# Stick-breaking heads: the weight product as two fp32r products instead of one in fp32

## The chip, the cores and the metric

The kernel runs on one core of one Trainium2 chip. The metric is the device time of one execution in microseconds (us), as the median of several runs. The names of the engines below: PE is TensorE (matmuls), DVE is VectorE, ACT is ScalarE, POOL is GpSimd, SP is SyncE. PE writes its products into PSUM, eight banks of 512 fp32 columns for each of the 128 partitions; DVE and ACT read and write PSUM and SBUF.

## The reference, cut to what matters

Two transformer blocks run one after the other over 512 tokens of width 1024. The second has a mixer of three kinds of heads; the change is in its six stick-breaking heads of width 64:

```
z = einsum('bqhd,bkhd->bhqk', q_blk, k) * scale
log_beta = log_sigmoid(z)
log_stay = where(before, log_sigmoid(-z), 0.0)
tail = cumsum(log_stay, axis=3, reverse=True) - log_stay
weight = where(before, exp(log_beta + tail), 0.0)
out = einsum('bhqk,bkhd->bqhd', weight, v)
...
y = concatenate([y_a, y_b, y_c], axis=-1) @ w_out
x = x + (1.0 + gate1) * y
```

Here `before` keeps the keys that lie ahead of the query. `y_b` are these six heads (384 columns); `y_a` comes from a gating branch, `y_c` from dilated-window heads. A feed-forward layer follows.

## The kernel before

Activations lie transposed in SBUF, channels on partitions and the 512 tokens along the free dimension. A product of near-fp32 accuracy is made of fp32r products (fp32r is the one-pass format of PE): each operand is split into a high part (rounded to fp32r, a CAST) and a low part (the rest, a subtract), and `mm3` (lines 163 to 166) adds three products, high by high, low by high and high by low. `split_to` (lines 119 to 133) makes the two parts: the high part on ACT (line 126) or on DVE (line 124), the low part on DVE (line 131). Weights come from HBM on SP's queue in `slab` and are split there (`whi` on ACT, line 154, `wlo` on DVE, line 156).

The heads come in three pairs. `stick` (from line 1009) does one head. Keys lie on partitions in four blocks j of 128, and only queries at or behind the block are computed, so the blocks have 512, 384, 256 and 128 columns. They lie in three PSUM tiles `z` (t = 0: 512 columns; t = 1: 384; t = 2: 256 + 128). For each tile, from t = 2 to t = 0:

- PE makes z (two fp32r products for each block, line 1026, and a mask, line 1028).
- ACT makes softplus in three steps (Abs, line 1031; Exp and Ln through `act`, line 231), DVE finishes it (line 1034) and splits it (`sph`, `spl`, lines 124 and 131).
- DVE adds up what lies in later blocks (lines 1040 and 1043), ACT and DVE split it (`lah`, `lal`).
- PE subtracts the running sums from z (products with `negtri` and `negone`, line 1054).
- ACT takes Exp into an fp32 tile `w`, and PE multiplies it with the values, in fp32, into a bank `o` that both heads of the pair share (line 1060). The stationary operand is a window of 128 columns with one head's 64 value columns and 64 zeros, so that each head adds to its own 64 partitions.

After a pair, `split_to` turns `o` into two fp32r parts for the output product. The values tile `vn` is made by `values` (lines 822 to 828) from the bank of a token-wise product; it also holds the values of one dilated group.

Between the heads stand "fills": the output product of `y_a` and `y_c` (`w_out_ac`, eight blocks of 15 fp32r matmuls with 512 columns, `mm3` lines 164 to 166) and the splitting of two slabs of the next layer's weights. `FILL` says behind which head each fill stands in the program. The order on each engine isn't the program's: a scheduler sets it when the kernel is built, by its own estimate of times, by the tiles' buffers and by program order; on the chip each engine then runs its list in that order and waits by semaphores. The PSUM pool of this phase has one bank `ps`, six `z` and one `o`. `last_phase` (from line 1180) then adds the product of `y_b` with `w_out_b`: first three blocks of 512 columns, each with its three k steps in a row, then `gemm_last` in halves of 256 columns.

Of the kernel before, what the change touches and what calls it, by code (L numbers as in the profile page):

```python
# [22 lines left out]
T = 512  # L23
# [24 lines left out]
class Builder:  # L48
# [773 lines left out]
    def values(self, ps, npair, pool, tag):  # L822
# [4 lines left out]
        self.nc.scalar.copy(v[:, :, 0::2, :], ps[:, :npair * P].rearrange("p (r s c) -> p r s c", s=2, c=64))  # L827
        return t

    def by_rest(self, parts):  # L830

        cols = []
        for i, ps in enumerate(parts):
            t = self.t("sq", 2, self.tmp)
            (self.nc.vector.tensor_copy if i else self.nc.scalar.copy)(
                t.rearrange("p (c m) -> p c m", c=4), ps.rearrange("p (m c) -> p c m", c=4))
            cols.append(t)
        for c in range(4):
            ps = self.ps() if c % 2 == 0 else ps
            half = ps[:, 256 * (c % 2):256 * (c % 2) + 256]  # L840
            for i, t in enumerate(cols):
                self.nc.tensor.transpose(half[:, i * P:i * P + P], t[:, c * P:c * P + P], self.ident)
            yield half
# [74 lines left out]
    def dilated_values(self, vn, vp, y_pool):  # L918
        nc = self.nc
# [50 lines left out]
        for g in (1, 2, 0):  # L970
            out = self.ps() if g == 2 else self.ps("st", 1)
            banks = [[(b, b) for b in range(4)]] if g else [[(0, 0), (1, 0), (1, 1)], [(2, 1), (2, 2), (3, 2), (3, 3)]]
            for h in range(2):
                p, f = probs[2 * g + h], lse[g][:, 4 * h:4 * h + 4]
                if g:
                    v = p.rearrange("p (b c) -> p b c", b=4)
                    tt(v, v, f.unsqueeze(2).to_broadcast([P, 4, P]), ALU.mult)
                else:
                    o = 0
                    for b in range(4):  # L980
                        n = 128 if b == 0 else 256
                        nc.vector.tensor_scalar(p[:, o:o + n], p[:, o:o + n], f[:, b:b + 1], None, ALU.mult)
                        o += n
            o = 0
            for bank in banks:
                n = len(bank) * P
                pts = []
                for h in range(2):
                    ps = self.ps("sc", 3)
                    for i in range(len(bank)):  # L990
                        nc.tensor.transpose(ps[:, i * P:(i + 1) * P], probs[2 * g + h][:, o + i * P:o + i * P + P],
                                            self.ident)
                    pt = self.t("sq" if h else "rb", 2, self.tmp)
                    (nc.vector.tensor_copy if h else nc.scalar.copy)(pt[:, :n], ps[:, :n])
                    for i, (b, j) in enumerate(bank):
                        pts.append((b, j, h, pt[:, i * P:(i + 1) * P]))
                o += n
                for b in sorted({b for b, _ in bank}):
                    mine = [x for x in pts if x[0] == b]
                    for i, (_, j, h, pt) in enumerate(mine):  # L1000
                        v = self.window(vp[j], g - 1, h) if g else self.window(vn[j], 3, h)
                        nc.tensor.matmul(out[:, b * P:(b + 1) * P], v, pt, start=i == 0, stop=i == len(mine) - 1)
            if g:
                ys[g] = self.split(out.rearrange("p (c m) -> p c m", c=4), y_pool, "y", view=perm)
            else:
                ys[g] = self.split(out, y_pool, "y")
        return ys

    def stick(self, qh, ql, k, v, pair, h, out):


        nc = self.nc
        where = {0: (0, 0), 1: (1, 0), 2: (2, 0), 3: (2, 256)}
        sp = [None] * 3

        later = [None] * 4
        for t in (2, 1, 0):
# [44 lines left out]

    def part(self, n, tag, whole, rest, name, dt=F32R):

        return self.ph.tile([P, n], dt, tag=f"{tag}{n}", name=name, bufs=whole if n == T else rest)

    def mixer(self, stat):

# [5 lines left out]
        with ExitStack() as ctx:  # L1074
# [4 lines left out]
            with stat as cx:  # L1079
# [38 lines left out]
                kt_pool = self.pool("kt", 3, ctx, side="right")  # L1118
                self.ph = ph
                with cr:  # L1120
                    qk = self.dilated_qk(self.dilated_in(xs, 1), cos, sin, 1)
                    for g, after in ((1, 2), (2, 0), (0, None)):
                        mine, start = qk, self.tc.tile_snap_priority()
                        if after is not None:
                            parts = self.dilated_in(xs, after)
                        else:
                            vn = [self.values(ps, 4, vn_pool, "vn") for ps in
                                  self.gemm_tok(self.dr["w_vn"], xs, T, 2, lambda t, b: t[:, b * P:(b + 1) * P])]
                        with self.before(start):
                            self.dilated_scores(g, *mine)  # L1130
                        if after is not None:
                            qk = self.dilated_qk(parts, cos, sin, after)
                bqk = []
                for pr in range(3):
                    q, k = self.pair(self.dr["w_bqk"], pr, xs)
# [11 lines left out]
            with ExitStack() as ce:  # L1147
                self.psum = self.pool("psum_e", 6, ce, space=PSUM)
                self.ph = self.pool("ph_c2", 1, ce)
                self.bufs = {"ps": 1}  # L1150
                add = self.add_gated(16)
                ready = []

# [6 lines left out]
                        self.gemm(self.dr["w_out_ac"], y_a + y_c, add, (abs(i),), m=2 * abs(i), tag="z" if i < 0 else "ps")  # L1160

                for pr in range(3):
                    out = self.ps("o", 1)
                    for h in range(2):
                        self.stick(*bqk[pr][h], vn, pr, h, out)
                        for i in FILL[2 * pr + h]:
                            fill(i)
                    if pr < 2:
# [5 lines left out]
                    self.split_to(out, *y_b[-1])  # L1174
                for i in FILL[6]:
                    fill(i)
        self.bufs = {}
# [2 lines left out]
    def last_phase(self, y_b, wq, held, first, wf0, ctx):  # L1180

        with ctx:
# [9 lines left out]
            for m, k, pool in ((0, 3, ()), (3, 3, ()), (6, 2, (wq, D))):  # L1192
# [183 lines left out]
```

## Time and profile before

| | us |
|---|---|
| median of 3 runs | 1729.18 |
| lowest and highest run | 1727.09, 1729.4 |
| the profiled execution, whole | 1730.88 |
| its span in the trace | 1729.1 |
| PE busy | 1708.1 (99%) |
| DVE busy | 1123.8 (65%) |
| ACT busy | 709.3 (41%) |
| POOL busy | 54.0 (3%) |

The rows below come from this one execution; it lies 1.7 us above the median. Times in them are microseconds from the span's start. A row of the timeline tells when an instruction began and how long it lasted; the next on the same engine may begin before that end, since engines are pipelined, so what an instruction costs in a dense row is the distance of two starts. The heads' phase lies from 1268.5 to 1333.3 us.

### The profile page before, as it was taken

The numbers are of one execution on the slowest core, as the hardware profiler recorded it, in microseconds if no ns is written. First come the engines' busy times: TensorE is split into PE (matmuls) and PEld (weight loads), VectorE is DVE, ScalarE is ACT, GpSimd is POOL, SyncE is SP. The second block draws the span as 40 slices with busy tenths as digits, with TensorE's granted clock in tenths as the row PEclk, the third lists the DMA queues.
The fourth block names the chain that finished last, engine by engine and source line by source line (L and its number), as shares of the span: only waits on it lengthen the run. The fifth ranks groups of instructions, "written<-read, shape, count | busy, mean of one in ns | idle before, by whom it ended". The sixth has DMA issues, their size and how long they took to land.

```text
span 1729.1 us, 20582 instructions
## 1 busy us (share of the span) xinstructions
PE 1708.1 (99%) x8175; PEld 1426.2 (82%) x8175; DVE 1123.8 (65%) x1756; ACT 709.3 (41%) x1078; POOL 54.0 (3%) x97
## 2 busy tenths in 40 slices
PE   9999999999999999999999999999999999999998
PEld 7888887888888788887888888987788988888887
DVE  5655699537756478879963775676577766536644
ACT  4323334314434355543431443543466444314432
POOL 0000000000000110000000000012100000000000
PEclk9999999999999999999999999999999999999999
DMA  6222464222222232236423222414323022222221
GB/s 233 98 97 98 143 237 172 88 103 98 90 101 102 74 98 74 92 112 246 178 100 107 98 90 99 149 53 130 102 63 107 28 75 97 100 107 98 90 101 66
DMA packets 39472, 189.99 MB, mean 110 GB/s; under 512 B 5584, under 2 KB 6608, under 8 KB 27216
## 3 DMA queue, kind: packets, MB, share of 16 engines
q1 hardware_dynamic: 36000, 180.94, 29.9%
q0 software_dynamic: 2656, 6.30, 1.5%
q8 instruction: 64, 1.05, 0.2%
q10 hardware_dynamic: 720, 1.44, 0.2%
q14 instruction: 32, 0.26, 0.0%
HBM read 180.27 MB, written 2.10 MB: 105 GB/s over the span
## 4 chain that ended last, share of the span: by engine, by line
PE 88%; DVE 6%; DMA 3%; issue 1%; ACT 1%; DVEq 0%; POOLq 0%; POOL 0%; SPq 0%; ACTq 0%
PE ps L164 27%; PE ps L165 27%; PE ps L166 26%; DMA ada<-w_ada 2%; DVE ada L483 2%; DVE wlo L156 1%; DVE cv L283 1%; PE pt L164 1%; PE pt L165 1%; PE o L1060 1%; PE pt L166 1%; PE sc L674 1%; PE z L1054 1%; PE sc L907 0%; PE z L1026 0%
## 5 line engine op out<-in xcount | busy, mean ns | idle before, releaser
L165 PE MATMUL ps<-xsh,wlo 128*128 128x512 f32 (+1 forms) x1416 | 546.0, 387 | 1.7 <-DVE wlo L156 1.4
L166 PE MATMUL ps<-xsl,whi 128*128 128x512 f32 (+1 forms) x1416 | 542.6, 385 | 0.0
L164 PE MATMUL ps<-xsh,whi 128*128 128x512 f32 (+1 forms) x1416 | 540.9, 387 | 0.8 <-ACT xsh L128 0.6
L154 ACT CAST whi<-raw 128x1024 fp32r<-128x1024 f32 (+6 forms) x281 | 296.5, 1060 | 466.6 <-PE ps L166 390.1
L156 DVE TENSOR_TENSOR wlo<-raw,whi 128x1024 fp32r<-128x1024 f32 (+4 forms) x282 | 346.8, 1233 | 91.9 <-ACT whi L154 90.6
L165 PEld LDWEIGHTS ps<-xsh,wlo 128*128 128x128 f32 x1416 | 267.3, 189 | 58.0 <-DVE wlo L156 5.0
L164 PEld LDWEIGHTS ps<-xsh,whi 128*128 128x128 f32 x1416 | 267.2, 189 | 55.6 <-ACT xsh L128 1.4
L166 PEld LDWEIGHTS ps<-xsl,whi 128*128 128x128 f32 x1416 | 265.8, 188 | 52.5
L165 PE MATMUL ps<-hidh,wlo 128*128 128x512 f32 (+1 forms) x658 | 241.4, 367 | 0.0
L164 PE MATMUL ps<-hidh,whi 128*128 128x512 f32 (+1 forms) x658 | 241.3, 368 | 0.0
L166 PE MATMUL ps<-hidl,whi 128*128 128x512 f32 (+1 forms) x658 | 241.3, 367 | 0.0
L283 DVE SCALAR_TENSOR_TENSOR cv<-e,par,cv 128x511 f32<-128x511 f32 x192 | 142.0, 746 | 2.2 <-ACT cv L279 0.4
L164 PEld LDWEIGHTS ps<-hidh,whi 128*128 128x128 f32 x658 | 123.9, 188 | 20.6
L165 PEld LDWEIGHTS ps<-hidh,wlo 128*128 128x128 f32 x658 | 123.6, 188 | 20.7 <-DVE wlo L156 0.2
L166 PEld LDWEIGHTS ps<-hidl,whi 128*128 128x128 f32 x658 | 123.7, 188 | 20.4
L288 DVE TENSOR_TENSOR h<-ps,h 128x512 f32<-128x512 f32 (+1 forms) x67 | 44.4, 666 | 120.9 <-PE ps L166 120.6
L283 DVE SCALAR_TENSOR_TENSOR cv<-ps,par,cv 128x511 f32<-128x511 f32 (+1 forms) x88 | 65.5, 749 | 79.3 <-ACT cv L281 77.7
L423 DVE TENSOR_TENSOR e<-ps,rb 128x512 f32<-128x512 f32 x88 | 60.1, 687 | 55.9 <-PE ps L166 55.9
L126 ACT CAST hidh<-cv 128x512 fp32r<-128x512 f32 x66 | 40.8, 619 | 129.3 <-DVE cv L431 129.3
L279 ACT ACTIVATE cv<-e,par 128x512 f32<-128x512 f32 x96 | 69.0, 721 | 31.1 <-DVE e L423 30.4
L429 ACT ACTIVATE si<-cv 128x512 f32<-128x512 f32 x66 | 41.7, 632 | 84.9 <-DVE cv L283 84.6
L292 DVE SCALAR_TENSOR_TENSOR h<-ps,mod,h 128x512 f32<-128x512 f32 (+1 forms) x38 | 24.2, 637 | 60.7 <-PE ps L166 60.6
(355 smaller groups left out, 1822.7 us busy)
## 6 DMA issues: line engine op xcount, KB each, us to landing
raw<-w_up SPq DMA_DIRECT2D x65, 1024.0 KB, 4.7
raw<-w_down SPq DMA_DIRECT2D x48, 704.0 KB, 4.0
ada<-w_ada SPq DMA_DIRECT2D x48, 512.0 KB, 4.4
raw<-a_w_in SPq DMA_DIRECT2D x9, 1024.0 KB, 4.7
raw<-a_w_out SPq DMA_DIRECT2D x4, 1024.0 KB, 4.7
raw<-w_o SPq DMA_DIRECT2D x4, 1024.0 KB, 5.1
raw<-w_uq SPq DMA_DIRECT2D x4, 768.0 KB, 4.2
raw<-w_cqk SPq DMA_DIRECT2D x3, 1024.0 KB, 4.8
```

Of the source, the lines that this page charges most:

```text
L126: nc.scalar.copy(vh, src)
L154: nc.scalar.copy(hi[:, :m], raw[:, s])
L156: nc.vector.tensor_tensor(lo[:, :m], raw[:, s], hi[:, :m].bitcast(F32), ALU.subtract)
L164: mm(ps, wh, xh, start=first, stop=False)
L165: mm(ps, wl, xh, start=False, stop=False)
L166: mm(ps, wh, xl, start=False, stop=last)
L279: nc.scalar.activation(y, x, AF.Identity, scale=self.p(w, 2 * n + i))
L283: nc.vector.scalar_tensor_tensor(y[:, k:], x[:, :T - k], self.p(w, (2 - k) * n + i), y[:, k:], ALU.mult, ALU.add)
L288: self.nc.vector.tensor_tensor(self.h[m][:, s], ps, self.h[m][:, s], ALU.add)
L423: nc.vector.tensor_tensor(e, ps, rb, ALU.mult)
L429: nc.scalar.activation(st["s"], y, AF.Silu)
L483: nc.vector.scalar_tensor_tensor(w, w, 1.0, ca, ALU.mult, ALU.mult, accum_out=self.mod[:, i:i + 1])
```

## The change

The values of the six heads get a tile of their own, `vs`, in which each pair of heads has five blocks of 64 columns: low part of the first head, its high part, zeros, high part of the second, its low part. ACT casts the high parts, DVE subtracts the low parts. A window of 128 columns is then either "both" (high and low part side by side) or "high" (high part and zeros). The weights are split too: Exp is written back into the PSUM tile `z`, ACT casts it to `wxh`, and DVE subtracts `wxl`. For each block, PE does two fp32r products, `both` with `wxh` and `high` with `wxl`, in place of one in fp32. A head's sum then fills its whole bank: high-part products on its own 64 partitions, the low part's on the other 64. So each head has a bank `o` of its own (two of them, and five `z` for six), and `stick_out` folds each: ACT copies the other half to SBUF, POOL's queue moves it by DMA to the head's own partitions, DVE adds the bank's own half, and `split_to` splits the sum. In `last_phase` the first three blocks now run with k outside, so that the last pair is used last. The tiles `sph` and `spl` have 2 and 4 buffers for 3 and 6, and two unused tiles are taken from the pool first, which sets which banks `o` gets.

```diff
+    def values_stacked(self, ps, npair, pool):
...
+        nc.gpsimd.memset(f[:, :, 2:3, :], 0.0)
+        nc.scalar.copy(at(t)[:, :, 1:4:2, :], src)
+        nc.vector.tensor_tensor(at(t)[:, :, 0::4, :], src, f[:, :, 1:4:2, :], ALU.subtract)
...
+        both, high = (320 * pair + o for o in ((192, 128) if h else (0, 64)))
...
-            sh, sl = (self.part(n, "s", 3, 6, name) for name in ("sph", "spl"))
+            sh, sl = (self.part(n, "s", 2, 4, name) for name in ("sph", "spl"))
...
-            w = self.part(n, "w", 2, 4, "w", F32)
-            self.act(w, ps[:, :n], AF.Exp)
+            wh, wl = (self.part(n, "w", 2, 5, name) for name in ("wxh", "wxl"))
+            self.act(ps[:, :n], ps[:, :n], AF.Exp)
+            self.split_to(ps[:, :n], wh, wl)
...
-                first = h == 0 and j == 3
-                nc.tensor.matmul(out[:, j * P:], self.window(v[j], pair, h), w[:, o:o + n], start=first, stop=True,
-                                 skip_group_check=not first)
+                for c, w in ((both, wh), (high, wl)):
+                    first = j == 3 and c == both
+                    nc.tensor.matmul(out[:, j * P:], v[j][:, c:c + P], w[:, o:o + n], start=first, stop=True,
+                                     skip_group_check=not first)
...
+    def stick_out(self, outs, hi, lo):
...
+        rest, u = self.t("sq", 2, self.tmp), self.t("acc", 1, self.tmp)
+        for h, out in enumerate(outs):
+            own, other = slice(64 * h, 64 * h + 64), slice(64 - 64 * h, 128 - 64 * h)
+            nc.scalar.copy(rest[other], out[other])
+            nc.gpsimd.dma_start(u[own], rest[other])
+            nc.vector.tensor_tensor(u[own], u[own], out[own], ALU.add)
+        self.split_to(u, hi, lo)
...
-            for m in range(3):
-                ps = self.ps()
-                for k in range(3):
-                    self.mm3(ps, *weights[m][k], *y_b[k], k == 0, k == 2)
-                add(m, ps)
+            ps = [self.ps() for _ in range(3)]
+            for k in range(3):
+                for m in range(3):
+                    self.mm3(ps[m], *weights[m][k], *y_b[k], k == 0, k == 2)
+            for m in range(3):
+                add(m, ps[m])
```

How the order moves is seen at three places. The names in the rows are the tiles above; a row's line numbers are those of its own kernel.

PE in the fourth head, where the correction of its 384-column tile begins, before:

```order
L1054 MATMUL z<-lah,negoner 128x256
L1054 MATMUL z<-lal,negoner 128x256
L1054 MATMUL z<-sph,negtrir 128x384
L1054 MATMUL z<-spl,negtrir 128x384
L164 MATMUL ps<-yh,whi 128x512
L165 MATMUL ps<-yh,wlo 128x512
L166 MATMUL ps<-yl,whi 128x512
L164 MATMUL ps<-yh,whi 128x512
```

And PE after the change, at the same place of the fourth head:

```order
L1068 MATMUL z<-lah,negoner 128x256
L1068 MATMUL z<-lal,negoner 128x256
L1068 MATMUL z<-sph,negtrir 128x384
L1068 MATMUL z<-spl,negtrir 128x384
L1076 MATMUL o<-wxh,vs 128x128
L1068 MATMUL z<-lah,negoner 128x384
L1076 MATMUL o<-wxl,vs 128x128
L1076 MATMUL o<-wxh,vs 128x256
```

Before, the fills in `ps` stand between the tiles of nearly all heads; now all six fills that go into `ps` stand ahead of the same place in the third head (row 181 of 324 of the phase), 90 rows without a fill follow, and the last two fills (in `z`) come beside the sixth head.

DVE at the end of the heads' phase, before (`h` takes the fills' results, `wlo` are weights of the next phase):

```order
L156 TENSOR_TENSOR wlo<-raw,whi 128x1024
L156 TENSOR_TENSOR wlo<-raw,whi 128x1152
L131 TENSOR_TENSOR lal<-rb,lah 128x256
L131 TENSOR_TENSOR lal<-rb,lah 128x384
L292 SCALAR_TENSOR_TENSOR h_91<-z,mod,h_91 128x512
L156 TENSOR_TENSOR wlo<-raw,whi 128x1152
L131 TENSOR_TENSOR wloq<-o,whiq 128x512
L156 TENSOR_TENSOR wlo<-raw,whi 128x768
```

And after:

```order
L131 TENSOR_TENSOR spl<-sq,sph 128x512
L1091 TENSOR_TENSOR acc<-acc,o 64x512
L156 TENSOR_TENSOR wlo<-raw,whi 128x1024
L131 TENSOR_TENSOR lal<-rb,lah 128x384
L131 TENSOR_TENSOR wxl<-z,wxh 128x384
L156 TENSOR_TENSOR wlo<-raw,whi 128x1152
L131 TENSOR_TENSOR wxl<-z,wxh 128x512
L1091 TENSOR_TENSOR acc<-acc,o 64x512
L131 TENSOR_TENSOR wloq<-acc,whiq 128x512
L156 TENSOR_TENSOR wlo<-raw,whi 128x768
```

Subtracts of the weights (`wxl`) and the adds of the folded heads (`acc`) have come in, the last of them behind the last weights' split.

ACT behind the first pair, after the change (`sq<-o` is the copy for the fold of the second head; `sq<-z` is the Abs of the fourth head's 512-column tile, and it goes into the buffer of `sq` that the copy was in):

```order
L1089 COPY sq<-o 64x512
L231 ACTIVATE z<-z 128x384
L126 CAST wxh<-z 128x384
L1045 ACTIVATE sq<-z 128x512
L126 CAST lah<-rb 128x384
```

Before, no copy stood there, and the two buffers of `sq` held softplus tiles alone.

## Rows read from the trace of the kernel before

**Rows 1.** The page: busy time of each engine; the granted clock of PE in 40 slices.

```profile
PE 1708.1 (99%) x8175; PEld 1426.2 (82%) x8175; DVE 1123.8 (65%) x1756; ACT 709.3 (41%) x1078; POOL 54.0 (3%) x97
PEclk9999999999999999999999999999999999999999
```

**Rows 2.** Windows of the heads' phase: us; PE, PEld, DVE, ACT, POOL busy; clock.

```profile
1268.50:1303.00 34.50, 34.03 (x186) 28.81 (x186) 26.70 (x57) 26.88 (x57) 0.00 (x0) 1.00 0.06 20
1303.00:1333.30 30.30, 30.15 (x147) 24.12 (x146) 24.08 (x43) 21.56 (x40) 0.00 (x0) 1.00 0.27 87
```

**Rows 3.** PE by shape, 1268.5 to 1333.3: count, busy us, mean ns, idle before.

```profile
L165 PE MATMUL ps<-yh,wlo 128*128 128x512 f32 x30 | 11.8, 392 | 0.0
...
L1060 PE MATMUL o<-w,vn 128*128 128x128 f32 x12 | 2.4, 281 | 0.5 <-ACT w L231 0.5
```

**Rows 4.** Timeline of PE in the heads: start, duration, instruction.

```profile
1313.73 1.02 PE L1060 MATMUL o<-w,vn 128*128 128x512 f32 x2
...
1314.83 0.39 PE L1026 MATMUL z<-wloq,kt 128*128 128x512 f32 x1
...
1330.69 0.39 PE L1054 MATMUL z<-sph,negtrir 128*128 128x512 f32 x1
1330.92 0.40 PE L1054 MATMUL z<-spl,negtrir 128*128 128x512 f32 x1
...
1333.33 0.79 PE L164 MATMUL ps<-whiq,whi 128*128 128x512 f32 x1
```

**Rows 5.** DVE by shape in the same stretch.

```profile
L1034 DVE SCALAR_TENSOR_TENSOR rb<-z,rb 128x384 f32<-128x384 f32 x12 | 6.7, 556 | 7.2 <-ACT rb L231 5.1 <-PE z L1028 2.1
```

**Rows 6.** Timeline of DVE in the heads.

```profile
1270.04 0.69 DVE L131 TENSOR_TENSOR yl<-st,yh 128x512 fp32r<-128x512 f32 x1 [2.54 <-ACT yh L126]
1272.82 0.56 DVE L1034 SCALAR_TENSOR_TENSOR rb<-z,rb 128x384 f32<-128x384 f32 x1 [2.09 <-PE z L1028]
...
1290.01 0.56 DVE L1034 SCALAR_TENSOR_TENSOR rb<-z,rb 128x384 f32<-128x384 f32 x1
1290.48 0.55 DVE L131 TENSOR_TENSOR spl<-rb,sph 128x384 fp32r<-128x384 f32 x1
...
1302.65 0.68 DVE L131 TENSOR_TENSOR spl<-sq,sph 128x512 fp32r<-128x512 f32 x1
1303.25 0.55 DVE L131 TENSOR_TENSOR spl<-rb,sph 128x384 fp32r<-128x384 f32 x1
...
1331.71 1.36 DVE L156 TENSOR_TENSOR wlo<-raw,whi 128x1152 fp32r<-128x1152 f32 x1 [1.00 <-ACT whi L154]
```

**Rows 7.** ACT by shape in the heads.

```profile
L231 ACT ACTIVATE w<-z 128x384 f32<-128x384 f32 x12 | 5.9, 492 | 3.1 <-PE z L1054 3.1
...
L126 ACT CAST lah<-rb 128x384 fp32r<-128x384 f32 x6 | 3.1, 513 | 2.7 <-DVE rb L1043 2.7
...
L126 ACT CAST whiq<-o 128x512 fp32r<-128x512 f32 x2 | 1.2, 588 | 0.5 <-PE o L1060 0.4
```

**Rows 8.** DMA issues of 64 partitions by 512, POOL's queue: us to landing.

```profile
whiq<-whiq POOLq DMA_DIRECT2D x6, 128.0 KB, 2.3
...
kt<-acc POOLq DMA_DIRECT2D x6, 128.0 KB, 3.8
```

**Rows 9.** Timeline of PE behind the values' token-wise product.

```profile
1216.77 0.49 PE L907 MATMUL sc<-whiq 64*128 64x128 f32 x2
...
1219.03 0.50 PE L164 MATMUL ps<-xsh,whi 128*128 128x512 f32 x1
```

**Rows 10.** DVE, a subtract over 64 partitions from PSUM, by shape, 1214 to 1240.

```profile
L649 DVE TENSOR_TENSOR acc<-ps,kt 64x512 fp32r<-64x512 f32 x2 | 1.4, 689 | 2.3 <-ACT kt L648 2.3
```

**Rows 11.** Windows in the next phase, where the granted clock falls.

```profile
1352.00:1354.00 2.00, 1.20 (x10) 0.97 (x8) 1.80 (x5) 0.94 (x3) 0.00 (x0) 1.00 0.00 0
1354.00:1356.00 2.00, 1.99 (x12) 1.97 (x12) 1.86 (x6) 0.89 (x2) 0.87 (x1) 0.64 0.00 0
1356.00:1358.00 2.00, 2.00 (x11) 2.00 (x11) 1.93 (x6) 1.09 (x3) 0.00 (x0) 0.50 0.00 0
```

More of the change, by code (lines that the diff above doesn't have):

```diff
@@ L828, in values @@
         return t
+    def values_stacked(self, ps, npair, pool):
+        nc = self.nc
+        t = pool.tile([P, npair * 320], F32R, tag="vs", name="vs", bufs=4)
+        at = lambda t: t.rearrange("p (r s c) -> p r s c", s=5, c=64)
+        src = ps[:, :npair * P].rearrange("p (r s c) -> p r s c", s=2, c=64)
+        f = at(t.bitcast(F32))
+        nc.gpsimd.memset(f[:, :, 2:3, :], 0.0)
+        nc.scalar.copy(at(t)[:, :, 1:4:2, :], src)
+        nc.vector.tensor_tensor(at(t)[:, :, 0::4, :], src, f[:, :, 1:4:2, :], ALU.subtract)
+        return t
     def by_rest(self, parts):
@@ L1000, in dilated_values @@
                     for i, (_, j, h, pt) in enumerate(mine):
-                        v = self.window(vp[j], g - 1, h) if g else self.window(vn[j], 3, h)
+                        v = self.window(vp[j], g - 1, h) if g else self.window(vn[j], 0, h)
                         nc.tensor.matmul(out[:, b * P:(b + 1) * P], v, pt, start=i == 0, stop=i == len(mine) - 1)
@@ L1054, in stick, with part @@
                         nc.tensor.matmul(ps[:, o + b:o + m], tri, s, start=False, stop=True, skip_group_check=True)
-            w = self.part(n, "w", 2, 4, "w", F32)
-            self.act(w, ps[:, :n], AF.Exp)
+            wh, wl = (self.part(n, "w", 2, 5, name) for name in ("wxh", "wxl"))
+            self.act(ps[:, :n], ps[:, :n], AF.Exp)
+            self.split_to(ps[:, :n], wh, wl)
             for j in js:
                 o, n = where[j][1], T - j * P
-                first = h == 0 and j == 3
-                nc.tensor.matmul(out[:, j * P:], self.window(v[j], pair, h), w[:, o:o + n], start=first, stop=True,
-                                 skip_group_check=not first)
-    def part(self, n, tag, whole, rest, name, dt=F32R):
-        return self.ph.tile([P, n], dt, tag=f"{tag}{n}", name=name, bufs=whole if n == T else rest)
+                for c, w in ((both, wh), (high, wl)):
+                    first = j == 3 and c == both
+                    nc.tensor.matmul(out[:, j * P:], v[j][:, c:c + P], w[:, o:o + n], start=first, stop=True,
+                                     skip_group_check=not first)
+    def part(self, n, tag, whole, rest, name):
+        return self.ph.tile([P, n], F32R, tag=f"{tag}{n}", name=name, bufs=whole if n == T else rest)
+    def stick_out(self, outs, hi, lo):
+        nc = self.nc
+        rest, u = self.t("sq", 2, self.tmp), self.t("acc", 1, self.tmp)
[5 more added lines that the diff above has]
+        self.split_to(u, hi, lo)
     def mixer(self, stat):
@@ L1117, in mixer @@
                 yc_pool = self.pool("y_c", 6, ctx, side="right")
-                kt_pool = self.pool("kt", 3, ctx, side="right")
                 self.ph = ph
@@ L1126, in mixer @@
                         else:
-                            vn = [self.values(ps, 4, vn_pool, "vn") for ps in
-                                  self.gemm_tok(self.dr["w_vn"], xs, T, 2, lambda t, b: t[:, b * P:(b + 1) * P])]
+                            vn, vs = [], []
+                            for ps in self.gemm_tok(self.dr["w_vn"], xs, T, 2,
+                                                    lambda t, b: t[:, b * P:(b + 1) * P]):
+                                vs.append(self.values_stacked(ps, 3, vn_pool))
+                                vn.append(self.values(ps[:, 3 * P:], 1, vn_pool, "vn"))
                         with self.before(start):
@@ L1132, in mixer @@
                             qk = self.dilated_qk(parts, cos, sin, after)
+                kt_pool = self.pool("kt", 3, ctx, side="right")
                 bqk = []
@@ L1149, in mixer @@
                 self.ph = self.pool("ph_c2", 1, ce)
-                self.bufs = {"ps": 1}
+                self.bufs = {"ps": 1, "z": 5}
+                self.ps("z")
+                self.ps("ps")
                 add = self.add_gated(16)
@@ L1162, in mixer @@
                 for pr in range(3):
-                    out = self.ps("o", 1)
+                    outs = []
                     for h in range(2):
-                        self.stick(*bqk[pr][h], vn, pr, h, out)
+                        outs.append(self.ps("o", 2))
+                        self.stick(*bqk[pr][h], vs, pr, h, outs[h])
                         for i in FILL[2 * pr + h]:
@@ L1173, in mixer @@
                     y_b.append([t[:, o:o + T] for t in y01])
-                    self.split_to(out, *y_b[-1])
+                    self.stick_out(outs, *y_b[-1])
                 for i in FILL[6]:
```

## The prediction

> **What bounds the kernel now.** [...] PE is busy for 34.03 of 34.50 us and then for 30.15 of 30.30, at the full clock; DVE for 26.70 and 24.08, ACT for 26.88 and 21.56 [rows 2]. The phase is PE's: in 64.8 us PE waits for well under 1 us (0.5 of it for a weight tile from ACT [rows 3]). But DVE is no bystander. It has 50.8 us of work there, and its first softplus row begins only at 1272.82, 4.3 us after the phase [rows 6]. From there to the end of its last weights' split, at 1331.71 + 1.36 = 1333.07 [rows 6], are 60.25 us. One row of 0.7 us lies ahead of 1272.82 [rows 6], so 50.1 us of the work are in these 60.25, and DVE stands idle for 10.1 us in between, half of it for a next head's Ln from ACT [rows 5]. That number decides the case.
>
> **The change part by part.** *PE's product.* Six heads have 128 + 256 + 384 + 512 = 1280 columns each. A fp32 product of 512 columns and one fp32r product of as many take 1314.83 - 1313.73 = 1.10 us together; the fp32r one alone takes 1330.92 - 1330.69 = 0.23 [rows 4]. So fp32 costs 0.87, nearly four times as much, and two fp32r products 0.46. Per 512 columns 0.41 us go, for 6 x 1280 / 512 = 15 such units 6.2 us; PE's 64.2 us of work in the phase become 58.0.
>
> *DVE's subtracts and adds.* Before, Exp went straight into the product's operand. Now each tile needs a `wxl` subtract from PSUM: twelve of 384 columns, six of 512. Its nearest row is the softplus row of the same shape that also reads PSUM, 0.556 us long [rows 5], but in a dense stretch the next start follows after 1290.48 - 1290.01 = 0.47, and for 512 columns after 1303.25 - 1302.65 = 0.60 [rows 6]. That is 12 x 0.47 + 6 x 0.60 = 9.2 us. Six adds over 64 partitions by 512 columns: the nearest row, a subtract of that shape, lasts 0.689 [rows 10], as long as the 0.68 of a full one of 512 columns [rows 6], so 0.60 each, 3.6 us. DVE gains 12.8 us of work and has 62.9 from 1272.82 on. [...]
>
> *ACT's casts and copies.* Eighteen casts and six copies, at most 12 x 0.513 + 6 x 0.588 + 6 x 0.588 = 13.2 us by the casts of these sizes [rows 7]; Exp itself keeps its size (0.492 for 384 columns [rows 7]), now with PSUM as target, which no row shows: taken at the same price, with 0.1 either way for each of 18, 1.8 us that ACT can hide. ACT comes from 48.4 to at most 61.6, just under DVE.
>
> *The buffers.* The fold's copy and the fourth head's Abs share a buffer of `sq`: Abs has to wait until the copy's DMA has landed, 2.3 to 3.8 us [rows 8], and two instructions of about 0.5 us stand in between. ACT stands for 1.3 to 2.8 us there, once, and all behind it with it. Five `z` banks for six, each held longer by the cast and the subtract, and the smaller `sph` and `spl` work the same way: they make waits, not work. I count them with DVE's waits below.
>
> *The values.* Four subtracts of 384 columns on DVE (2 us), and ACT's four copies become eight. PE's next use of these banks comes at 1219.03, and from 1216.77 it has products of the dilated heads to do [rows 9]: 2.3 us of cover, against a cast, a copy and a subtract of about 1.5 us. Cost nothing; if the cover were gone, 1 us. POOL's memsets of `vs` now stand behind DMA issues of the dilated heads, far ahead of their first reader: nothing. SP's order stays as it was.
>
> *The end of the phase.* PE can't leave before the last `wxl`, and that stands behind the last weights' split on DVE (second place of the order). Then the fold: PE 0.23 and its pipe 0.17, ACT's copy 0.59 [rows 7], the DMA 2.3 [rows 8], DVE's add 0.68, ACT's cast 0.59, in sum 4.6 us until the high part is there. PE has the 18 products of the first two pairs ahead, 18 x 0.23 = 4.1, two halves (0.2) and the last product itself, 4.5. The reversed loop hides the fold all but for 0 to 0.5 us (1.5 more if the DMA takes 3.8): 0.4.
>
> *The sum.* If DVE never waited from 1272.82 on, its last `wxl` would end at 1272.8 + 62.9 = 1335.7, 2.6 us behind the 1333.07 of before, and PE starts the next phase 0.3 behind that, as it does now at 1333.33 [rows 4]. That is the floor. Now the waits. PE's list up to the third head (first place of the order: 180 rows) holds all six fills, 90 x 0.23 = 20.7 us, and 90 head products; those that stay as they are cost PE 58.0 - 120 x 0.23 - 6.9 = 23.5 us for 156, or 0.15 each, the 90 here cost 13.5, in sum 34.2 us, and are done at 1302.7. DVE has 51 rows up to there, at 50.8 / 100 = 0.51 us [rows 2] 26.0 us, begun at 1272.8: it has time left, 1302.7 - 1272.8 - 26.0 = 3.9 us, and waits for PE. Behind that place DVE still has 62.9 - 26.0 = 36.9 us, PE only 58.0 - 34.2 = 23.8: PE waits for DVE. There I let DVE run dense but for 1.0 us, the shorter part of ACT's standing for the buffer of `sq`: 1302.7 + 36.9 + 1.0 = 1340.6, 7.5 us later than before. With the fold, 7.9. So the 6.2 us that PE saves are lost, since another engine ends last, and 7.9 us more. Both ends: nothing waits, 2.6 + 0.4 = +3.0; all 10.1 us of waits stay and the DMA is the slow one, 2.6 + 10.1 + 1.9 = +14.6.
>
> The profiled execution would go from 1730.88 to 1738.8. The median lies 1.7 below: 1729.18 + 7.9 = **1737.1**.
>
> **The rivals.** *DVE closes up.* The same mechanism without waits, +3.0: 1732.2, which no measurement can tell from 1729.2, so not slower. For it: in the fills' stretch DVE may run ahead of PE's list. Against it: PE's order puts the fills there first, and DVE's rows need PE's. It decides if less than 0.4 us of the 3.9 and the 1.0 stays.
>
> *PE still decides, faster.* 1729.18 - 6.2 = 1723.0. DVE would have to do its 123 rows in 58.6 - 4.3 = 54.3 us, 0.44 us each without one wait; they take 0.51 now [rows 2]. It decides from there down. I see no row for that, but the order on all engines is new, and half of DVE's splits could turn out cheaper in it.
>
> *All waits stay.* Both ACT (61.6 with 1.3 to 2.8 of standing) and DVE run in order and wait for each other; before, DVE waited 30.30 - 24.08 = 6.2 us in the second window [rows 2]. The same behind 1302.7 gives 6 us more: 1743.
>
> [...]
>
> **How the numbers follow.** Forecast 0.53; all waits stay 0.12; the clock 0.08; DVE closes up 0.17; PE decides 0.10. A measurement can tell about 0.2% of this kernel, 3.5 us: same is 1725.7 to 1732.6. Faster 0.10; same 0.20, the dense case and a small share of the forecast; slower 0.70. The range reaches up to 1745, over the two dear cases, and down to 1729: the dense case, less 1.7 if the slow-clock stretch of the next phase goes away and 1.7 for the spread of the runs. Below it lies the faster case, above it a few in a hundred.
>
> **What would show it.** In the profile after: PE's heads' phase lasts some 72 us for 64.8, its busy share behind the fills is well under 90%, with idle ahead of `wxl` and `wxh` products ended by DVE and ACT; DVE is busy for about 63 us of it, over 90% in the second part; the product itself is some 6 us cheaper; the first product of the next phase starts near 1341; the third pair's product there waits under 1 us. Wrong would be: PE busy throughout (then DVE's additions were cheaper or the waits went), or a granted clock of 0.5 in the heads.

## The result, and the profile after

The changed kernel is slower: 1748.9 us median (1746.24 to 1750.23, 4 runs) against 1728.13 (1727.03 to 1729.4, 4 runs) of the kernel before on the same chip, a ratio of 1.0117 with a 95% interval of 1.0104 to 1.0129. That is +20.8 us; forecast was +7.9, with a range up to 1745.

The page after, busy time and PE's granted clock in 40 slices (compare [rows 1]):

```profile
PE 1711.0 (98%) x8175; PEld 1429.5 (82%) x8175; DVE 1139.0 (65%) x1784; ACT 719.2 (41%) x1106; POOL 57.1 (3%) x107
...
PEclk9999999999999999999999999999997999999999
```

One slice, 1308 to 1352 us, has lost clock (its digit is 7 for 9): the last part of the heads and the hand-over to the next phase. To compare kernels I cut each trace at three events: the first score product of the first head, the first product of the next phase, and the first product of the feed-forward layer. The windows after (start and end, length, busy time of PE, PEld, DVE, ACT, POOL with counts, PE's granted clock, DMA share, GB/s): the whole heads' phase; DVE's two stretches, cut at the 1302.7 of the forecast; and four windows of 5 us.

```profile
1267.85:1343.55 75.70, 66.52 (x324) 54.98 (x325) 62.75 (x121) 57.29 (x119) 2.58 (x5) 0.93 0.20 56
1271.55:1302.70 31.15, 30.71 (x162) 26.46 (x160) 26.91 (x53) 22.87 (x48) 0.52 (x1) 1.00 0.18 54
1302.70:1342.91 40.21, 31.47 (x140) 24.55 (x139) 35.84 (x70) 31.71 (x66) 2.07 (x4) 0.87 0.23 60
1308.00:1313.00 5.00, 2.00 (x6) 0.85 (x5) 4.00 (x10) 3.96 (x9) 0.00 (x0) 0.92 0.01 3
1313.00:1318.00 5.00, 4.87 (x19) 4.78 (x20) 3.39 (x9) 3.73 (x9) 0.52 (x1) 0.50 0.11 26
1343.00:1348.00 5.00, 2.04 (x5) 1.12 (x4) 0.20 (x1) 0.58 (x1) 0.52 (x1) 0.50 0.57 213
1348.00:1353.00 5.00, 4.46 (x11) 3.49 (x12) 2.14 (x3) 1.35 (x2) 0.00 (x0) 0.50 0.20 46
```

The heads before, cut the same way, and the last row of PE's fills there:

```profile
1269.14:1333.33 64.19, 63.58 (x328) 52.32 (x326) 50.78 (x99) 48.44 (x97) 0.00 (x0) 1.00 0.16 52
1329.53 0.39 PE L166 MATMUL z<-yl,whi 128*128 128x512 f32 x1
```

The heads take 75.7 us; before they took 64.2. From there to the feed-forward layer it is 26.9 us for 20.7. That is +11.5 and +6.2, in sum 17.7, where the forecast had +7.5 and +0.4. (The spans differ by 15.4 only. A second profile of the kernel before, e8 below, has 1727.4, 17.1 less than after, and the profiled run of after was the fastest of its four.)

The hand-over shows the second loss best. PE after (start, duration, what it is; in brackets the time for which PE stood ahead of it, and who ended that):

```profile
1342.96 0.79 PE L1076 MATMUL o<-wxl,vs 128*128 128x512 f32 x1
1343.55 0.63 PE L164 MATMUL ps<-whiq,whi 128*128 128x512 f32 x1
1343.98 0.63 PE L165 MATMUL ps<-whiq,wlo 128*128 128x512 f32 x1
1344.41 0.63 PE L166 MATMUL ps<-wloq,whi 128*128 128x512 f32 x1
1348.54 0.79 PE L164 MATMUL ps<-whiq,whi 128*128 128x512 f32 x1 [3.51 <-DVE acc L1091]
1349.13 0.63 PE L165 MATMUL ps<-whiq,wlo 128*128 128x512 f32 x1
```

and the last fold meanwhile, on ACT, POOL and DVE:

```profile
1343.79 0.58 ACT L1089 COPY sq<-o 64x512 f32<-64x512 f32 x1 [1.61 <-PE o L1076]
...
1344.66 0.52 POOL L1090 DMA_DIRECT2D acc<-sq  x1 [10.49 <-ACT sq L1089]
...
1347.80 0.69 DVE L1091 TENSOR_TENSOR acc<-acc,o 64x512 f32<-64x512 f32 x1 [4.89 <-DMA acc<-sq]
1349.17 0.69 DVE L131 TENSOR_TENSOR wloq<-acc,whiq 128x512 fp32r<-128x512 f32 x1 [0.68 <-ACT whiq L126]
```

Of the 18 products that were to cover the fold, three run. The fourth waits for the fold's own add, though it needs nothing of the last pair: it is the first product into the second `ps` bank, and that is the bank in which the last head's sum lies. In the built program the next phase takes banks 1, 7, 6, 5, 4, 3, 2 in this order, and the sums of first and second heads lie in 6 and 7. Ahead of the stop and behind it, products of 512 columns start 0.43 us apart, not the 0.23 of [rows 4]: the granted clock is 0.50 there, from 1343 to 1353.

All kernels but e8, each with its ratio to runs of the kernel before on its own chip (0.1% is 1.7 us), the two stretches, and DVE's busy time in the heads:

| kernel | ratio (95%) | heads, us | to feed-forward, us | DVE, us |
|---|---|---|---|---|
| before | 1 | 64.2 | 20.7 | 50.8 |
| after | 1.0117 (1.0104 to 1.0129) | 75.7 | 26.9 | 62.8 |
| e1 banks | 1.0085 (1.0070 to 1.0100) | 74.8 | 23.0 | 63.4 |
| e2 last pair unfolded | 1.0089 (1.0073 to 1.0104) | 74.2 | 22.8 | 62.2 |
| e3 no subtracts | 1.0083 (1.0065 to 1.0101) | 68.5 | 27.9 | 54.0 |
| e4 banks, splits on POOL | 1.0075 (1.0056 to 1.0093) | 74.5 | 23.0 | 64.0 |
| e5 banks, fills spread | 1.0074 (1.0054 to 1.0094) | 74.9 | 22.1 | 62.0 |
| e6 the same, other places | 1.0121 (1.0103 to 1.0139) | 79.7 | 23.4 | 63.2 |
| e7 before + subtracts | 1.0037 (1.0024 to 1.0049) | 71.3 | 21.9 | 59.4 |
| e9 banks, PE busy in the middle | 1.0069 (1.0052 to 1.0086) | 74.8 | 22.3 | 63.5 |
| e10 and at the end | 1.0068 (1.0053 to 1.0083) | 74.7 | 22.3 | 63.5 |
| e11 banks, no folds | 1.0085 (1.0068 to 1.0101) | 75.5 | 21.2 | 60.2 |
| e12 e11, no subtracts | 1.0010 (0.9999 to 1.0021) | 66.0 | 21.7 | 51.2 |
| e13 banks, no casts | 1.0105 (1.0086 to 1.0125) | 77.3 | 25.8 | 62.9 |
| e14 e12, no casts | 1.0001 (0.9991 to 1.0011) | 66.0 | 20.3 | 50.7 |
| e15 before + casts | 1.0017 (1.0008 to 1.0027) | 65.9 | 20.7 | 52.1 |
| e16 before, two products | 1.0011 (1.0002 to 1.0021) | 64.5 | 21.2 | 50.7 |
| e17 before, small buffers | 1.0014 (1.0004 to 1.0023) | 65.6 | 20.7 | 51.3 |
| e18 e16, fills spread | 0.9971 (0.9960 to 0.9983) | 61.2 | 20.3 | 50.2 |

### The profile page after: what moved, and what is told of

It reads as the page before. It is cut to its first block, busy times and chain, and to the rows that moved or that the text cites. A ratio compares the mean times of both kernels' runs of the same rounds, so it can differ in the third digit from the quotient of the medians.

```text
span 1744.5 us, 20654 instructions
## 1 busy us (share of the span) xinstructions
PE 1711.0 (98%) x8175; PEld 1429.5 (82%) x8175; DVE 1139.0 (65%) x1784; ACT 719.2 (41%) x1106; POOL 57.1 (3%) x107
## 4 chain that ended last, share of the span: by engine, by line
PE 90%; DVE 4%; DMA 2%; issue 2%; ACT 1%; DVEq 0%; POOLq 0%; POOL 0%; SPq 0%; ACTq 0%
PE ps L164 28%; PE ps L165 28%; PE ps L166 28%; DMA ada<-w_ada 1%; DVE wlo L156 1%; PE pt L164 1%; DVE ada L483 1%; PE pt L165 1%; PE pt L166 1%; PE sc L674 1%; DMA acc<-sq 1%; PE sc L920 0%; PE pt L685 0%; DMA raw<-w_uq 0%; PE z L1068 0%
## 5 line engine op out<-in xcount | busy, mean ns | idle before, releaser
L154 ACT CAST whi<-raw 128x1024 fp32r<-128x1024 f32 (+5 forms) x281 | 296.7, 1060 | 482.1 <-PE ps L166 399.6
L156 DVE TENSOR_TENSOR wlo<-raw,whi 128x1024 fp32r<-128x1024 f32 (+5 forms) x282 | 346.9, 1233 | 94.2 <-ACT whi L154 92.6
L165 PEld LDWEIGHTS ps<-hidh,wlo 128*128 128x128 f32 x658 | 123.6, 188 | 20.8
L166 PEld LDWEIGHTS ps<-hidl,whi 128*128 128x128 f32 x658 | 123.7, 188 | 20.3
L292 DVE SCALAR_TENSOR_TENSOR h<-ps,mod,h 128x512 f32<-128x512 f32 (+1 forms) x38 | 24.1, 638 | 63.0 <-PE ps L166 62.8
```

The source lines that it names most:

```text
L154: nc.scalar.copy(hi[:, :m], raw[:, s])
L156: nc.vector.tensor_tensor(lo[:, :m], raw[:, s], hi[:, :m].bitcast(F32), ALU.subtract)
L165: mm(ps, wl, xh, start=False, stop=False)
L166: mm(ps, wh, xl, start=False, stop=last)
L292: self.nc.vector.scalar_tensor_tensor(self.h[m][:, s], ps, self.mod[:, gate + m:gate + m + 1], self.h[m][:, s], ALU.mult, ALU.add)
```

## Experiments: the end of the heads

**e1**, other banks, the same instructions in the same order (`total(h)` takes a tile of tag `o0` or `o1` with one buffer, so the sums come to lie in banks 2 and 0):

```diff
-                self.ps("z")
-                self.ps("ps")
+                total(1)
+                self.ps("ps")
+                total(0)
+                self.ps("z")
```

> The changed kernel with the same instructions in the same order on every engine; only the banks of PSUM are dealt out otherwise, so that the two heads' sums lie in the banks that the next phase takes last (in the changed kernel the sum of each second head lies in the bank of that phase's second product). [...] Rival B (the fold itself holds the phase, the third pair comes at the same time either way): under 1 us less, 1748 to 1749.

1742.27 us, 1.0085: by the ratios 5.5 us less than after, where rival B had under 1. The stretch behind the heads falls from 26.9 to 23.0, the heads from 75.7 to 74.8. PE at the same place:

```profile
1342.92 0.63 PE L164 MATMUL ps<-whiq,whi 128*128 128x512 f32 x1
...
1344.63 0.59 PE L165 MATMUL ps<-whiq,wlo 128*128 128x512 f32 x1
1345.05 0.40 PE L166 MATMUL ps<-wloq,whi 128*128 128x512 f32 x1
...
1349.55 0.50 PE L164 MATMUL ps<-whiq,whi 128*128 128x512 f32 x1 [1.14 <-ACT whiq L126]
```

The 18 products run without a stop, 0.43 us apart up to 1345.05 and 0.23 from there (the granted clock is 0.80 from 1343 to 1348 and 1.00 from 1348 to 1353), and the third pair's products wait 1.14 us for the fold. So the bank costs 3.9 us of the 6.2 behind the heads; of the 2.3 left the fold's wait is half.

**e2**, the last pair split without its fold:

```diff
+        if not fold:
+            return self.split_to(outs[1], hi, lo)
```

> The changed kernel, but the last pair's sums are not folded: copy, DMA and add of its two heads are left out and the second head's bank is split as it stands, so the last pair's values are wrong. Theory A (the chain of copy, DMA, add at the end of the heads, 4.9 us until the add and 3.5 us of PE's standing for it, is exposed): 3.5 to 6 us less than the changed kernel, 1743 to 1745.5. Rival B (DVE's and the clock's loss within the heads is nearly all): under 1.5 us less.

1743.54 us, 4.8 us less than after by the ratios, as A had it: here the bank is free early.

## Experiments: the work of DVE and ACT

**e3**, no subtracts (`nc.scalar.copy(wh, ps[:, :n])` and `wl = wh` for the split).

> The changed kernel without the 18 subtracts for the low part of the weights: the second product reads the high part once more, so that TensorE's work stays the same and the result is wrong. Theory A (VectorE's additional 9 us set the end of the heads): VectorE falls from 62.8 to 53.6 us, TensorE with 58 us ends last again, the heads end 8 to 12 us earlier, 1737 to 1741. [...]

1741.58 us, by the ratios 5.9 us less than after, short of A's 8 to 12. The heads are 7.2 us shorter than after, 68.5. Part of it is lost again at the hand-over, where the banks are those of after: PE stands 5.8 us for the last fold's add, which gets its DMA 5.1 us after the copy.

```profile
1337.03 0.39 PE L166 MATMUL ps<-wloq,whi 128*128 128x512 f32 x1
1343.21 0.79 PE L164 MATMUL ps<-whiq,whi 128*128 128x512 f32 x1 [5.79 <-DVE acc L1092]
```

**e7**, the other way round: the kernel before with the subtracts alone.

```diff
             self.act(w, ps[:, :n], AF.Exp)
+            rest = self.ph.tile([P, T], F32, tag="r", name="wxl", bufs=1)[:, :n]
+            nc.vector.tensor_tensor(rest, ps[:, :n], w, ALU.subtract)
```

> The kernel before with 18 additional subtracts on VectorE, of the shapes of the changed kernel's (PSUM minus SBUF, 384 and 512 columns), whose result nobody reads; the fp32 product stays. VectorE has 59 to 60 us of work in the heads, TensorE 64. Theory A (the additional work on VectorE lengthens the phase by itself, since VectorE works in order and its waits don't go away): 4 to 9 us above before. Rival B (it goes into VectorE's 10 us of waits as long as TensorE is the one with more work): under 2.5 us above before.

1734.54 us, +0.37%; the heads are 7.1 us longer with 8.6 us more work on DVE. Theory A's number: hardly any of it goes into the 10 us of DVE's waits, though PE still has 64 us of work. But the 7.1 us aren't shown to be DVE's work alone. The scheduler gave e7 another order too: the last of the fills is issued 11.4 us ahead of the next phase and not 3.8, and behind it PE and DVE stand in turn (DVE once for 2.6 us).

```profile
1327.03 0.39 PE L166 MATMUL z<-yl,whi 128*128 128x512 f32 x1
...
1338.45 1.42 PE L164 MATMUL ps<-whiq,whi 128*128 128x512 f32 x1
```

What such an order costs where DVE has no more work is seen in e16 and e18 below. The subtract also holds each `z` bank longer; e15 and e17 below put 1.7 and 1.4 us on two changes of that kind.

**e11 and e12**, no folds (`stick_out` only splits `outs[1]`), then no subtracts either.

> e1 without any fold: copy, DMA and add of all three pairs are left out and one bank of each pair is split, so the heads' values are wrong. Theory D (VectorE stands in order for the folds' DMAs in the middle of the heads too, and the last fold is not quite covered): heads 2 to 5 us shorter than e1's 74.8, in all 3 to 6 us less than e1. Rival A (six adds of 0.6 us and nothing else): 3 us or less in all.

> e11 also without the 18 subtracts (the second product reads the high part once more; the result is wrong): what is left of the change is TensorE's 6.2 us less, ScalarE's 18 additional casts and the smaller buffers. Theory A (VectorE's 12.8 us were what took the gain away): VectorE has no more work than before, TensorE ends the heads, 58 to 62 us for 64.2, 1722 to 1727, faster than before. Rival D (the casts lengthen each tile's chain from Exp to product and TensorE stands for them): heads 65 us or more, 1728 or more, no faster than before.

e11: 1744.06 us, 1.0085 like e1. The hand-over is 1.8 us shorter, the heads are not: 3.2 us less work on DVE in another order of the lists. Theory D falls. e12: 1731.22 us, no difference from before. So with the subtracts and folds the loss goes, but TensorE's saving doesn't come out: heads 66.0, not the 58 to 62 of A. That is rival D's number; whether its reason, the casts, holds is what the next three ask.

**e13, e14 and e15** take ACT's casts out, or put them in. e13 lets Exp write the high part itself; e14 does so in e12; e15 adds the 18 copies to the kernel before:

```diff
-            self.act(w, ps[:, :n], AF.Exp)
+            self.act(ps[:, :n], ps[:, :n], AF.Exp)
+            nc.scalar.copy(w, ps[:, :n])
```

> e1 without ScalarE's 18 casts of the weights: Exp writes the high part itself, and VectorE's subtract keeps its shape but takes another value, so the result is wrong. VectorE's work and TensorE's stay as they are. Theory A (VectorE's 62.8 us set the end): heads 73 to 75 us as in e1, 1740 to 1742. Rival E (ScalarE, 58 us of work in order with VectorE, and the longer way from Exp to the product bring the waits in which VectorE stands): heads 69 to 72 us, 1735 to 1739.

> e12 without ScalarE's 18 casts as well (Exp writes the high part, both products read it; the result is wrong): of the change only TensorE's two products for one, the banks and the buffers are left, and the other engines have no more work than before. Theory A and E together (the work that the product brings to the other engines took its gain): TensorE's 58 us set the end, heads 59 to 63 us for 64.2, 1723 to 1727. Rival F (five banks for six and the smaller buffers hold the heads by themselves): heads 64 us or more, 1728 or more.

> The kernel before with 18 additional copies on ScalarE: Exp writes to PSUM, a copy of the same size brings it to the product's fp32 operand; nothing else is changed. ScalarE has 9.5 us more, about 58 in the heads, TensorE 64. Rival E (the longer chain and ScalarE's load cost time by themselves): 2.5 to 7 us above before. Theory A (they go into ScalarE's waits): under 2 us above before.

e13: 1746.09 us, heads 77.3 though ACT has 8 us less: E's gain isn't there, with the reserve that its order differs and the clock is 0.50 to 0.59 in parts of it. e15: heads +1.7, but +0.17% is 2.9 us (1.4 to 4.7), and that lies on both sides of the bound between A and E. e14: 66.0 as in e12, rival F's number. So the casts are worth some 3 us by e15 and nothing of the heads by e13 and e14, and something else takes TensorE's 6.2 us.

**e17**, the smaller buffers alone (`{"ps": 1, "z": 5}`, `sph` and `spl` with 2 and 4).

> The kernel before with the changed kernel's buffers: five z banks for six, two and four buffers of sph and spl for three and six; nothing else. Theory G: within 1.5 us of before, 1727.5 to 1730.5. Rival F: 2.5 to 6 us above before.

1731.83 us, 2.5 us above before (+0.14%, 0.7 to 4.0 us by the interval), at F's lower end; heads +1.4. The run doesn't part G from F, but either way the buffers are not enough for 6.

## Experiments: the clock, and the order of the fills

**e9**, e1 with idle products ahead of PE's two stops at 1309 to 1313, put into PE's list after the scheduler had made it:

```diff
+        places = [(tri(9, "sph")[0], 10, 3), (tri(9, "spl")[0], 1, 3)]
...
+                i = nc.tensor.matmul(total.outs[0].bass_ap, tri(3, "sph")[0].ins[1].bass_ap, q.ins[0].bass_ap, start=True, stop=True).ins
```

> e1 with 11 idle products (128x512, into the bank that the last fill has left, read by nobody) on TensorE's queue just ahead of the two products for which it stands 2.6 and 0.3 us at 1309 to 1313; every other instruction and its order as in e1. [...] Rival A (VectorE's own work sets the end whatever the clock): within 1 us of e1.

1740.60 us. The heads of e1 and of e9, each with the two windows concerned:

```profile
1268.16:1342.92 74.76, 65.55 (x327) 54.21 (x326) 63.43 (x122) 57.76 (x120) 2.58 (x5) 0.95 0.19 56
1308.00:1313.00 5.00, 2.15 (x6) 1.05 (x5) 3.94 (x9) 3.93 (x9) 0.00 (x0) 0.79 0.01 3
1313.00:1318.00 5.00, 4.91 (x19) 4.80 (x20) 3.36 (x9) 3.76 (x9) 0.52 (x1) 0.53 0.11 26
```

```profile
1267.38:1342.17 74.79, 66.69 (x338) 54.11 (x337) 63.48 (x122) 57.80 (x120) 2.58 (x5) 0.98 0.19 55
1308.00:1313.00 5.00, 4.28 (x19) 2.90 (x18) 4.37 (x10) 3.29 (x8) 0.00 (x0) 1.00 0.00 0
1313.00:1318.00 5.00, 4.42 (x21) 2.98 (x20) 3.31 (x8) 4.42 (x11) 0.52 (x1) 1.00 0.12 26
```

The granted clock is 1.00 in both windows, for 0.79 and 0.53 in e1, and the heads are as long as in e1, 74.79 for 74.76: rival A's number. PE's slow stretch lies in its own slack. (The time is 1.7 us under e1's, but on another chip, and the two ratios' intervals overlap; the heads decide.) PE is busy for 2.15 of the 5 us in which the clock falls in e1, and for 4.28, with no fall, in e9. Whether the fall costs time is another matter, and here it doesn't.

**e10** does the same at the end of the heads too, ahead of the last tile's products: `(tri(17, "lah")[0], 2, 5), (tri(17, "lal")[0], 6, 5), (of(5)[6], 4, 5)`.

> e9 with 12 more of these products ahead of the three places at which TensorE stands at 1336 to 1342 (0.6, 1.6 and 1.1 us), so that it comes to the next phase without a gap. Theory B (the clock): the granted clock stays at 1.00 in 1338 to 1348 too, the next phase's first products start 0.23 us apart and not 0.43, 1.5 to 3 us less than e9. Rival A: within 1 us of e9, since the third pair's products wait for the fold anyway and only wait longer.

1740.70 us, the same as e9: rival A. The granted clock is 1.00 in both windows from 1338 to 1348 (0.66 in e9), the next phase's products start 0.23 us apart (in e9 0.43 up to 1346.43), and the third pair's then wait 1.46 us, for none in e9. From the heads to the feed-forward layer it is 22.3 us in both. With the banks mended, the hand-over hangs on the fold, not on the clock.

**e4**, e1 with the low parts of the fills' weights on GpSimd (`nc.gpsimd.tensor_tensor` in `slab` during the heads).

> e1 with the low parts of the fills' weights (raw minus high part, 128x640 and 128x1024, ten tiles, about 9 us on VectorE within the heads) made by GpSimd, which has nothing else to do there. Theory A (VectorE's load sets the end): VectorE falls by 9 us, the heads end 6 to 10 us earlier than in e1, 1735 to 1740. Rival B (waits or TensorE's clock set the end, or GpSimd is so slow that the fills wait for its splits): within 2 us of e1 or above it.

1740.26 us, heads 74.5 for 74.8: no gain. But it doesn't speak for B, since DVE's busy time did not fall: 64.0 us, though seven tiles of splits (6.1 us by e1's rows) have left its list. POOL and DVE in e4:

```profile
1283.14 1.72 POOL L156 TENSOR_TENSOR wlo<-raw,whi 128x640 fp32r<-128x640 f32 x1 [4.67 <-ACT whi L154]
...
1283.47 1.80 DVE L131 TENSOR_TENSOR spl<-rb,sph 128x384 fp32r<-128x384 f32 x1
...
1286.91 0.56 DVE L131 TENSOR_TENSOR spl<-rb,sph 128x384 fp32r<-128x384 f32 x1
```

**e5 and e6** hold the fills back on PE's queue with an order edge (no wait) behind a later tile's triangular products:

```diff
+        self.marks, self.behind_ = [], {2: 3, 3: 6, 4: 9, 5: 12, 6: 14, 7: 16}
...
+                    with self.tc.issue_after(self.marks[self.behind_[m]]) if self.marks and m in self.behind_ else nullcontext():
```

(e6: `{1: 1, 2: 3, 3: 6, 4: 9, 5: 12, 6: 13, 7: 15}`; block number: place among the 18 tiles.)

> e1 with the eight fill outputs held back on TensorE's queue: each stands behind the triangular products of a later tile, one or two to a head instead of six within the first third of the phase. No work is added or left out. Theory A (VectorE's work alone sets the end of the heads): VectorE has the same 62.8 us, no more than 2 us less than e1, 1740 to 1743. [...]

> As e5, with the second fill one tile later and the last two one tile earlier, so that two fills lie ahead of the last head's middle tile. Theory A: within 2 us of e1, 1740 to 1743. [...]

1741.22 us, heads 74.9: A's number. But DVE isn't dense there either, 62.0 us of work in 74.9; the fills' places moved the waits and took none away. e6 is worse than e1, 79.7 for 74.8, which A did not have: a bad place costs 5 us.

**e8, e16 and e18** go back to the kernel before. e8 is it once more, for a second profile:

> [...]

1729.13 us, span 1727.4: the clock is 1.00 from 1353 to 1358 where [rows 11] had 0.64 and 0.50. The stretch at 0.50 is not in every run. (It lies at the first products of the feed-forward layer, which begin at 1354.04 before.) e16 makes the product alone cheaper, e18 also holds the fills back as e5 does:

```diff
+                for two in range(2):
+                    nc.tensor.matmul(out[:, j * P:], self.window(v[j], pair, h), w[:, o:o + n], start=first and two == 0, stop=True,
+                                     skip_group_check=not first or two > 0)
```

> The kernel before with two fp32r products of the same operands for each fp32 product of the weights, and nothing else: buffers, banks, adds and splits stay as they were (the result is wrong: every product counts twice and is rounded). TensorE has 58 us in the heads for 64.2, VectorE 50.8 and ScalarE 48.5 as before. Theory G (TensorE's 99% hid a ring of waits: the chain over ScalarE and VectorE is about as long as TensorE's list): heads 62 to 65 us, 1726 to 1730, no difference or a little less. Rival F (the smaller buffers of the changed kernel ate the gain in e14): heads 58 to 60.5 us, 1722 to 1725.

> e16 with the fill outputs held back on TensorE's queue as in e5, so that the last one stands ahead of the last tile's triangular products (the result is as wrong as e16's). Theory H (the order: the fills are drawn forward into the time that TensorE saves, and the last heads' chains stand without cover): heads 59 to 62.5 us, 1723 to 1727, faster than e16 by 3 us or more. Rival G (the chain over ScalarE and VectorE is as long as it was, wherever the fills stand): heads 63.5 us or more, 1728 or more.

e16: 1731.51 us, no gain at all from the cheaper product with nothing added: rival F falls, and the heads are in G's range. e18: 1724.23 us, 0.9971, the only kernel here that is faster than before. The windows of e16, then of e18:

```profile
1268.66:1333.19 64.53, 61.23 (x327) 52.56 (x326) 50.71 (x99) 48.66 (x97) 0.00 (x0) 0.96 0.21 68
1318.00:1323.00 5.00, 5.00 (x27) 4.28 (x26) 4.78 (x7) 3.99 (x7) 0.00 (x0) 1.00 0.19 29
1323.00:1328.00 5.00, 3.44 (x20) 2.49 (x18) 4.96 (x11) 1.95 (x3) 0.00 (x0) 1.00 0.51 167
1328.00:1333.00 5.00, 3.73 (x9) 2.49 (x10) 0.89 (x2) 1.49 (x3) 0.00 (x0) 0.53 0.60 210
```

```profile
1267.99:1329.20 61.21, 59.05 (x327) 51.61 (x326) 50.24 (x99) 48.58 (x97) 0.00 (x0) 1.00 0.18 54
1323.00:1328.00 5.00, 4.94 (x23) 3.87 (x22) 1.86 (x4) 1.68 (x3) 0.00 (x0) 1.00 0.68 192
```

In e16 PE is busy up to 1323 but for 0.5 us at 1277: it spends the time it saves on fills that the scheduler draws forward (the last is issued 9.8 us ahead of the next phase), and then has nothing to cover the last tiles' chains over ACT and DVE. In e18 the last fill stands there (2.8 us ahead), the granted clock is 1.00 from 1323 to 1333 (in e16 0.53 from 1328), and the heads are 3.3 us shorter than in e16, 3.0 shorter than before: H. PE is busy for 4.5 us less than before, 59.05 for 63.58. e18 leaves out the low parts and their work, so it is no replacement for either kernel; and the kernel before with its fills held back was not run, so how much of the gain over it is the product's stays open.

## Why the prediction was wrong

The direction was right, and half of its reason: the work that the change brings to DVE lengthens the heads (e3, e12). The other half, that this work is what takes TensorE's saving, was not (e16), and the size was off by two terms, DVE's waits in the second part and the end of the phase. Step by step:

- **DVE's added work:** 12.8 us, with 62.9 of work. Measured 62.75 - 50.78 = 12.0, and 62.75 in all. (At the rows' whole durations, 12 x 0.556 + 12 x 0.69, it would be 15.0.) Its main part, the 18 subtracts, is worth 7.2 us of the phase in e3 and 9.5 from e11 to e12. Right.
- **The waits up to 1302.7:** 3.9 us. Measured 31.15 - 26.91 = 4.2. Right.
- **The waits behind it:** "dense but for 1.0 us". Measured 40.21 - 35.84 = 4.4. This step failed by 3.4 us; with 0.3 more up to 1302.7 and 0.3 more from DVE's last row to the next phase's first product it is the 4 us that the heads miss. The larger waits, and the row of ACT that should have stood for the buffer of `sq` and follows the cast ahead of it without a gap:

```profile
1308.45 0.69 DVE L131 TENSOR_TENSOR wloq<-acc,whiq 128x512 fp32r<-128x512 f32 x1 [0.36 <-ACT whiq L126]
1309.78 0.69 DVE L1048 SCALAR_TENSOR_TENSOR sq<-z,sq 128x512 f32<-128x512 f32 x1 [0.63 <-ACT sq L231]
...
1316.22 0.56 DVE L131 TENSOR_TENSOR wxl<-z,wxh 128x384 fp32r<-128x384 f32 x1 [0.84 <-ACT wxh L126]
...
1318.26 0.68 DVE L1091 TENSOR_TENSOR acc<-acc,o 64x512 f32<-64x512 f32 x1 [1.02 <-DMA acc<-sq]
...
1342.22 0.69 DVE L131 TENSOR_TENSOR wxl<-z,wxh 128x512 fp32r<-128x512 f32 x1 [1.08 <-ACT wxh L126]
```

```profile
1305.47 0.48 ACT L126 CAST wxh<-z 128x384 fp32r<-128x384 f32 x1
1306.01 0.60 ACT L1045 ACTIVATE sq<-z 128x512 f32<-128x512 f32 x1
```

So the 1.0 was for a wait that didn't come, and those that came are mostly for the new rows' own inputs: 1.9 us for `wxh` from ACT and 1.0 for the fold's DMA. DVE kept nearly as much waiting as it had, 8.6 us for 10.1, as the rival "all waits stay" had it. Why it stays is open: without the folds (e11) or without the casts (e13) the heads were no shorter.
- **The end of the phase:** 0.4 us, measured 6.2. This is the larger miss. The sum of the fold's steps was 4.6 us until the high part; it took 1349.14 - 1342.96 = 6.2 (its DMA 3.1 from issue to add for 2.3). But the failed premise was the cover: I counted 18 products ahead of the third pair and never asked into which bank the fourth of them goes. It goes into bank 7, where the last head's sum lies, and waits for the fold's add. e1 prices that at 3.9 us.
- **The clock:** 0.08 stood on a loss by it, which was one of the range's two dear cases, and no run shows such a loss in the heads. It did fall there, to 0.50 from 1313 to 1318; in e9 it is 1.00 in this stretch, and the heads take 74.79 us for e1's 74.76, of which PE is busy for 65.55. At the hand-over it fell as well, and with the banks mended e10, at 1.00 for e9's 0.66, shows that it cost nothing there either: 22.3 us in both. What it cost behind the bank's stop in the changed kernel no run parts.
- **PE's saving:** I let the 6.2 us be lost to DVE. e16 shows that they would have been lost without DVE's work too, and e18 that the order of the fills holds a part of them, 3.3 us. Before, PE's 99% was no proof that PE alone bounds the phase.

The 17.7 us between the profiles, put together from the runs: at the hand-over 3.9 for the bank (after to e1), 1.6 for the rest of the fold (e10 to before; its wait there is 1.46) and 0.7 left over (e1 to e9); in the heads 7.2 for the subtracts (after to e3), 2.5 for the folds and the banks together (e3 to e12; the banks alone are 0.9, after to e1) and 1.8 that stay with both gone (e12 and e14 to before; the smaller buffers alone are 1.4). Taken out in the other order, the folds are worth nothing (e1 to e11) and the subtracts 9.5 (e11 to e12): DVE is in both, and the runs don't part them further. The medians show 3 us more than the profiles: after's profiled execution lies 2.7 below its median, and where the others lose that no profile shows.

## What to carry to other kernels

An engine that is busy for 99% of a stage need not be its only bound: take work from it alone, leave the rest as it is, and see whether time comes out, before other engines are asked to pay for it. When products are counted as cover for a transfer, look up into which PSUM bank each one goes and who reads that bank last. An in-order engine that gets more work need not lose its waits: here 8.6 of 10.1 us stayed. Charge them in full unless a row shows why they would go.

## What the runs showed of the hardware

In e4 a DVE subtract with two SBUF operands (`spl<-rb,sph`, 384 columns) begins at 1283.47, inside a GpSimd subtract over SBUF (1283.14, 1.72 us long), and takes 1.80 us, to 0.4 behind GpSimd's end, for 0.56 where none runs (at 1286.91). A DVE add of 128 columns over SBUF that begins at 1294.78, inside another (1294.53, 1.56 us), takes 1.45 for e1's mean of 0.285. A row that reads PSUM (`h<-ps,mod,h`, 512 columns, at 1288.66) lies wholly inside a third (1288.20, 1.58 us) and takes 0.74, for e1's mean of 0.746. The twelve `spl` rows of 384 columns take 0.87 us in the mean, for 0.55 in e1. With 11 products that nobody reads, PE's granted clock is 1.00 in e9 from 1308 to 1318, for 0.79 and 0.53 in e1, at no cost and no gain for the heads (74.79 us for 74.76).
